# The running sum of a width-31 convolution moves from SBUF to a PSUM bank

## The chip, the cores and the metric

The kernel runs on one core of a Trainium2 chip. The metric is device time in microseconds of one execution. A core has a matmul engine (TensorE, PE in the profile; PEld are its weight loads), a vector engine (VectorE, DVE), a scalar engine (ScalarE, ACT), a third engine for elementwise work (GpSimd, POOL) and a sequencer that here only issues DMAs (SP). Matmul results go to PSUM, of which the kernel uses eight banks of 128 partitions x 512 floats; all other tiles lie in SBUF.

## What is computed

One layer of a decoder trunk over 1024 tokens of width 1024, in float32:

```python
h = x * (1.0 + sc1) + sh1                       # shift and scale from an adaLN projection of c
proj = h @ w_in                                 # 5136 columns
conf_val, conf_gate, z, xbc, dt_raw = split(proj)
u = conf_val * sigmoid(conf_gate)
u = silu(layer_norm(causal_dwconv31(u) + b))    # depthwise, 31 taps, over 1024 channels
xbc = silu(causal_dwconv4(xbc))                 # depthwise, 4 taps
y = ssd_chunked(...)                            # Mamba-2 scan, chunks of 128, 16 heads in 4 groups
mix = concat([u, gated_rmsnorm(y, z)]) @ w_out
x = layer_norm(ALPHA * x + g1 * mix)
# then: a hierarchical mixture of 64 experts, two for each token, and a second layer norm
```

## The kernel before

Channels lie on the partitions and tokens along the free dimension. The tokens are worked through in two halves of 512 (`h` = 0 and 1). For each half, the projection runs in blocks of 128 columns: `proj` (L477) takes a PSUM bank and adds up 8 x 3 matmuls of 128x512 in it (L475; each float32 weight and input is split in a high and a low part, and three of the four products are taken). In the first half the weights come from HBM, are split by ACT (L448) and POOL (L449), and are stored as `wind`; the second half loads them from there.

A block of the wide convolution is in `conf_block` (L594). Its gate (`pg`) leaves its bank through ACT (L602), its value (`pv`) through DVE (L605), which also makes `u`. ACT sets the running sum `acc` to the last tap plus the bias (L609). Of the other 30 taps, the first three to five go to ACT and POOL (L614, L616); the rest are DVE's, one scalar_tensor_tensor for each (L620): `acc` = `u` shifted x weight + `acc`, 128x512. There are 16 such chains, eight in each half, 426 taps in all. POOL adds its part (L623).

PSUM is divided by tags: `mm` four banks, `ta` two, `ss` two. The projection's blocks use `mm`, and so do the adaLN accumulations (`ada`, L298 to L306): one of these runs for each third of that projection, two of them a few matmuls at a time between the blocks of the first half, each holding its bank from its first matmul to its last. The output projection (`out_mm`, L924) runs in four passes A to D of two token tiles; a pass needs four banks at once (`pms`), adds up 16 x 3 matmuls in each, and its banks are emptied by L969.

What is written here is a set of generators that are taken in turn; a scheduler then orders the instructions of each engine by its own model of their times. Each engine runs its list in order, so an instruction that waits holds up what stands behind it. After the output projection come routing tables and the experts, whose weights (`ring`) are streamed in.

## Time and profile before

| | |
|---|---|
| runs | 2160.04, 2157.35, 2159.57 us; median 2159.57 |
| profiled execution | 2157.99 us, of which the span of its instructions 2156.0 |
| mean granted clock of TensorE | 0.94 of full speed |
| busy: PE, DVE, ACT, POOL | 1826.5, 1073.0, 547.7, 619.1 us |
| L620, the taps | 426 instructions, 433.3 us busy, mean 1029 ns |
| written and read in HBM | 83.44 and 576.08 MB |

A busy engine is one with an instruction in flight. A stretch of the span is read by the engine that is fullest in it, and by who waits for whom; shares over the whole span mix stages with different limits. The name in front of an arrow is the tile that is written, those behind it are read. Where a wait is listed, the engine stood idle before that line until the other engine's line had finished.

### The profile page before, as it was taken

What the parts mean: (1) busy time and instruction counts of PE and PEld (TensorE: products, weight loads), DVE (VectorE), ACT (ScalarE), POOL (GpSimd) and SP (SyncE); (2) the same over time, 40 slices, a digit from 0 to 9 for tenths busy, and PEclk for the clock granted to TensorE, in tenths of its full rate; (3) what the DMA queues carried; (4) which work ended last, traced back from release to release, by engine and by line L of the source; (5) the groups of instructions that cost most, each with busy time, mean ns of one, the idle gap of its engine ahead of it and who ended that gap; (6) DMA issues with size and microseconds to landing.
All of it is one profiled execution on the core that took longest, in us unless ns stands there. A gap on an engine that the chain in (4) does not pass through costs nothing.

```text
span 2156.0 us, 23640 instructions
## 1 busy us (share of the span) xinstructions
PE 1826.5 (85%) x8135; PEld 1012.6 (47%) x8135; DVE 1073.0 (50%) x1796; ACT 547.7 (25%) x990; POOL 619.1 (29%) x440
## 2 busy tenths in 40 slices
PE   4897989689989999889678969989799897998784
PEld 1365656558667767767432313324234241433232
DVE  1499898977999999897830301000000000000036
ACT  0234535264344446443320000001000010000011
POOL 0345656651544346553510000100001000000014
PEclk7998999889989999999879999999999998999997
DMA  8877877646443425657489999899998999999964
GB/s 260 288 256 240 249 252 232 230 145 219 153 131 132 165 93 171 206 182 279 171 312 419 419 421 383 339 420 420 419 374 338 420 420 420 420 409 372 420 255 160
DMA packets 204278, 626.01 MB, mean 290 GB/s; under 512 B 25566, under 2 KB 91350, under 8 KB 157308
## 3 DMA queue, kind: packets, MB, share of 16 engines
q1 hardware_dynamic: 156080, 552.79, 66.9%
q10 hardware_dynamic: 36700, 46.51, 6.7%
q0 software_dynamic: 11376, 25.18, 3.3%
q8 instruction: 65, 1.06, 0.2%
q14 instruction: 57, 0.47, 0.1%
HBM read 576.08 MB, written 83.44 MB: 306 GB/s over the span
## 4 chain that ended last, share of the span: by engine, by line
PE 30%; DMA 26%; DVE 20%; issue 4%; ACT 2%; POOL 1%; ACTq 0%; SPq 0%; DVEq 0%; POOLq 0%
DMA ring<-in_expert_w_dram 24%; DVE acc L620 8%; PE mix L475 5%; PE h0h L1325 2%; PE h1h L1325 2%; PE ypl L1344 2%; PE yph L1344 2%; PE ypt L1344 1%; PE h1l L1325 1%; PE h0t L1325 1%; PE px L475 1%; PE h1t L1325 1%; PE h0l L1325 1%; DVE cy L694 1%; DVE ctl L950 1%
## 5 line engine op out<-in xcount | busy, mean ns | idle before, releaser
L620 DVE SCALAR_TENSOR_TENSOR acc<-u,cw,acc 128x512 f32<-128x512 f32 x426 | 433.3, 1029 | 17.5 <-ACT acc L609 13.5
L1290 POOL DMA_INDIRECT xg<-h2d,gidx x32 | 33.0, 1033 | 724.0 <-PE tph L1298 203.8
L475 PE MATMUL px<-hTh,wx_hl 128*128 128x512 f32 x512 | 175.3, 413 | 3.5 <-ACT wx_hl L448 3.0
L475 PE MATMUL mix<-wo_hl,cth 128*128 128x512 f32 x416 | 136.2, 421 | 14.9 <-DVE wo_hl L449 10.2
L1325 PE MATMUL h1s<-ring,xTs 128*32 128x512 f32 x512 | 99.3, 691 | 42.6 <-DMA ring<-in_expert_w_dram 42.6
L1344 PE MATMUL yps<-ring,hTs 128*32 128x512 f32 x512 | 109.5, 599 | 19.3 <-DMA ring<-in_expert_w_dram 16.9
L1331 DVE TENSOR_TENSOR s1s<-s1s,h1s 128x512 f32<-128x512 f32 x8 | 5.5, 688 | 223.2 <-PE h1s L1325 223.2
L475 PEld LDWEIGHTS px<-hTh,wx_hl 128*128 128x128 f32 x512 | 99.0, 195 | 36.0 <-ACT wx_hl L448 5.2
L475 PE MATMUL px<-hTl,wx_hl 128*128 128x512 f32 x256 | 105.1, 410 | 0.0
L475 PEld LDWEIGHTS mix<-wo_hl,cth 128*128 128x128 f32 x416 | 81.1, 199 | 38.4 <-DVE wo_hl L449 14.1
L449 POOL TENSOR_TENSOR wo_hl<-wo,wo_hl 128x512 fp32r<-128x512 f32 x52 | 76.1, 1473 | 60.5 <-ACT wo_hl L448 60.1
L305 PE MATMUL ada<-wada,cond 128*32 128x512 f32 x192 | 74.2, 673 | 21.9 <-DMA wada<-in_w_ada_dram 21.8
L475 PE MATMUL pg<-hTh,wg_hl 128*128 128x512 f32 x256 | 90.1, 419 | 1.9 <-ACT wg_hl L448 0.9
L1325 PE MATMUL h0s<-ring,xTs 128*32 128x512 f32 x512 | 75.6, 639 | 16.3 <-DMA ring<-in_expert_w_dram 16.3
L475 PE MATMUL pz<-hTh,wz_hl 128*128 128x512 f32 x256 | 86.2, 404 | 2.1 <-ACT wz_hl L448 1.1
L475 PE MATMUL mix<-wo_hl,ctl 128*128 128x512 f32 x208 | 80.3, 422 | 7.4 <-DVE ctl L950 7.3
L475 PE MATMUL pv<-hTh,wv_hl 128*128 128x512 f32 x256 | 85.7, 405 | 0.4 <-DVE h L514 0.4
L1325 PEld LDWEIGHTS h1s<-ring,xTs 128*32 128x32 f32 x512 | 22.0, 124 | 116.1 <-DMA ring<-in_expert_w_dram 75.3
L1349 DVE SCALAR_TENSOR_TENSOR ys<-yps,gslot,g_bc 128x512 f32<-128x512 f32 x16 | 12.0, 751 | 120.0 <-PE yps L1344 120.0
L448 ACT CAST wo_hl<-wo 128x512 fp32r<-128x512 f32 x104 | 63.1, 616 | 26.7 <-PE mix L475 14.7
L1344 PEld LDWEIGHTS yps<-ring,hTs 128*32 128x32 f32 x512 | 27.1, 109 | 87.5 <-issue 45.4
L1325 PE MATMUL h1l<-ring,xTl 128*64 128x512 f32 x256 | 63.1, 595 | 5.7 <-DMA ring<-in_expert_w_dram 5.7
(603 smaller groups left out, 3618.9 us busy)
## 6 DMA issues: line engine op xcount, KB each, us to landing
ring<-in_expert_w_dram SPq DMA_DIRECT2D x384, 1024.0 KB
wo<-in_w_out_dram SPq DMA_DIRECT2D x112, 256.0 KB
wada<-in_w_ada_dram SPq DMA_DIRECT2D x96, 256.0 KB
wind<-wx_hl SPq DMA_DIRECT2D x32, 512.0 KB
wx_hl<-wind SPq DMA_DIRECT2D x32, 512.0 KB
ybuf<-zeros ACTq DMA_DIRECT2D x8, 1024.0 KB
wind<-wg_hl SPq DMA_DIRECT2D x16, 512.0 KB
wind<-wv_hl SPq DMA_DIRECT2D x16, 512.0 KB
```

Of the source, the lines that this page charges most:

```text
L305: nc.tensor.matmul(pm[32 * j:32 * j + 32, :], lhs, wt, start=(k == 0), stop=(k == KT - 1), tile_position=(0, 32 * j))
L448: nc.scalar.copy(hi, wt)
L449: (eng or nc.gpsimd).tensor_tensor(lo, wt, hi, op=OP.subtract)
L475: nc.tensor.matmul(pt, lhs[a_], rhs[b_], start=(first and n == 0), stop=(last and n == 2))
L620: nc.vector.scalar_tensor_tensor(acc, u[:, j:j + HALF], cw[:, t, j:j + 1], acc, op0=OP.mult, op1=OP.add)
L694: nc.vector.scalar_tensor_tensor(acc, raw[:, j:j + HALF], sw[:, j, t:t + 1], acc, op0=OP.mult, op1=OP.add)
L950: nc.vector.tensor_tensor(cl, ck, ch, op=OP.subtract)
L1290: nc.gpsimd.indirect_dma_start(out=t_, out_offset=None, in_=h2d, in_offset=bass.IndirectOffsetOnAxis(ap=gcol, axis=0), bounds_check=T - 1, ...
L1325: nc.tensor.matmul(hp[a:b, :], xT[:, 4 * hf + k, a:b], w_[:, k, :], start=(hf + k == 0), stop=(hf + k == 4), tile_position=(0, a))
L1331: nc.vector.tensor_tensor(s1, s1, hps[1], op=OP.mult)
L1344: nc.tensor.matmul(yps[n][a:b, :], hT[:, 2 * hf + k, a:b], w_[:, k, 512 * n:512 * n + 512], start=(hf + k == 0), stop=(hf + k == 2), tile_ ...
L1349: nc.vector.scalar_tensor_tensor(y[:, half[n]], yps[n], gate, g2_bc[:, half[n]], op0=OP.mult, op1=OP.mult)
```

## The change

The pool `mm` goes from four banks to three, and a tag `ac` with one bank is new. In `taps`, the first DVE tap of a chain reads `acc` from SBUF and writes a tile in `ac`; the following ones read and write that tile; the last reads it and writes `acc` in SBUF. The transposes of the first half's start use `ac` for one of the banks that they had in `mm`. Passes A, C and D of the output projection take their fourth bank, or for C their second, from `ac`; B is as before.

```diff
--- before.py
+++ after.py
@@ -271,7 +271,11 @@
         wk = p0.enter_context(tc.tile_pool(name="wk", bufs=2, side="right"))
 
         def mm_bank(name):
-            return ps.tile([P, 512], F32, tag="mm", bufs=4, name=name)
+            return ps.tile([P, 512], F32, tag="mm", bufs=3, name=name)
+
+        def ac_bank(name):
+
+            return ps.tile([P, 512], F32, tag="ac", bufs=1, name=name)
 
         def ta_bank(name):
             return ps.tile([P, 512], F32, tag="ta", bufs=2, name=name)
@@ -482,7 +486,7 @@
 
         def make_h(h):
 
-            banks = [mm_bank] * 8 if h else [mm_bank] * 3 + [ta_bank] * 2 + [ss_bank] + [mm_bank] * 2
+            banks = [mm_bank] * 8 if h else [mm_bank] * 2 + [ac_bank] + [ta_bank] * 2 + [ss_bank] + [mm_bank] * 2
             hT = []
             tps = {}
 
@@ -591,6 +595,14 @@
             yield
             return v3(dt), v3(dtd), v3(cd), v3(nacs)
 
+        def taps(nm, acc, terms):
+
+            run_ = acc
+            for j, (v_, w_) in enumerate(terms):
+                to = acc if j == len(terms) - 1 else ac_bank(f"ac{nm}") if j == 0 else run_
+                nc.vector.scalar_tensor_tensor(to, v_, w_, run_, op0=OP.mult, op1=OP.add)
+                run_ = to
+
         def conf_block(h, hT, b):
             accs = []
             for s_ in range(2):
@@ -616,9 +628,7 @@
                         nc.gpsimd.tensor_tensor(side, side, tmp, op=OP.add)
                     else:
                         side = tmp
-                for j in range(m, 30):
-                    nc.vector.scalar_tensor_tensor(acc, u[:, j:j + HALF], cw[:, t, j:j + 1], acc,
-                                                   op0=OP.mult, op1=OP.add)
+                taps(f"{h}_{t}", acc, [(u[:, j:j + HALF], cw[:, t, j:j + 1]) for j in range(m, 30)])
                 if m:
                     nc.gpsimd.tensor_tensor(acc, acc, side, op=OP.add)
                 add_part(h, "m", MG, ME, t, acc)
@@ -924,7 +934,7 @@
         def out_mm(h, i0, cat_, banks):
 
             sl = slice(i0 * P, (i0 + 2) * P)
-            pms = [[bank(f"mix{h}_{i0 + i}_{n}") for n in range(2)] for i, bank in enumerate(banks)]
+            pms = [[bank(f"mix{h}_{i0 + i}_{n}") for n, bank in enumerate(pair)] for i, pair in enumerate(banks)]
             ks = list(range(16))
             if (h, i0) == (1, 2):
                 ks = ks[16 - NK:] + ks[:16 - NK]
@@ -1068,8 +1078,9 @@
         O2 = "LA B XA LB F C XB LC D XC LD XD".split()
         got = {}
         live = {}
-        passes = {"A": (0, 0, ok, (mm_bank, mm_bank)), "B": (0, 2, None, (ta_bank, mm_bank)),
-                  "C": (1, 0, ok, (mm_bank, ta_bank)), "D": (1, 2, None, (mm_bank, mm_bank))}
+        mm, ta, ma = (mm_bank, mm_bank), (ta_bank, ta_bank), (mm_bank, ac_bank)
+        passes = {"A": (0, 0, ok, (mm, ma)), "B": (0, 2, None, (ta, mm)),
+                  "C": (1, 0, ok, (ma, ta)), "D": (1, 2, None, (mm, ma))}
 
         def part(h, o_):
             k, n = o_[0], o_[1:]
```

The scheduler orders the whole program anew. On DVE, in the first half, where the convolution's blocks 2 and 3 meet (`acc_2` and `acc_3` are their sums in SBUF, `ac_2` and `ac_3` those in PSUM, `u_3` the input of block 3). Before:

```order
L605 SCALAR_TENSOR_TENSOR u_3_1247<-u_3_1247,pv_3_1249 128x512
L620 SCALAR_TENSOR_TENSOR acc_2_1101<-u_2_1071,cw,acc_2_1101 128x512
L607 COPY halo_u<-u_3_1247 128x30
L620 SCALAR_TENSOR_TENSOR acc_2_1101<-u_2_1071,cw,acc_2_1101 128x512
L620 SCALAR_TENSOR_TENSOR acc_3_1277<-u_3_1247,cw,acc_3_1277 128x512
L620 SCALAR_TENSOR_TENSOR acc_2_1101<-u_2_1071,cw,acc_2_1101 128x512
L620 SCALAR_TENSOR_TENSOR acc_3_1277<-u_3_1247,cw,acc_3_1277 128x512
```

And now:

```order
L617 SCALAR_TENSOR_TENSOR u_3_1250<-u_3_1250,pv_3_1252 128x512
L603 SCALAR_TENSOR_TENSOR ac_2_1113<-u_2_1073,cw,ac_2_1113 128x512
L619 COPY halo_u<-u_3_1250 128x30
L603 SCALAR_TENSOR_TENSOR ac_2_1113<-u_2_1073,cw,ac_2_1113 128x512 x9
L752 TENSOR_TENSOR xc_0_1431<-tr_0_1427,dt_778 128x256
L752 TENSOR_TENSOR xc_0_1461<-tr_0_1457,dt_778 128x256
L603 SCALAR_TENSOR_TENSOR acc_2_1103<-u_2_1073,cw,ac_2_1113 128x512
L603 SCALAR_TENSOR_TENSOR ac_3_1290<-u_3_1250,cw,acc_3_1280 128x512
```

Before, the taps of the two blocks alternate from here on; now block 2 is brought to its end, nine taps in a row, and block 3 begins behind its last.

On PE, later in the same half, where a piece of the second adaLN accumulation (`ada`) stands by the projection groups `px_10` and `px_14`. Before:

```order
L475 MATMUL px_10_2339<-hTl_4_421,wx_10_1_hl 128x512
L305 MATMUL ada_1580<-wada_52_2429,cond 32x512
L475 MATMUL px_14_2444<-hTh_0_393,wx_14_0_hl 128x512
L475 MATMUL px_10_2339<-hTh_4_417,wx_10_1_hl 128x512
L755 MATMUL y_1_2180<-dec_1_2166,xc_1_2176 64x128 x4
L764 MATMUL sp_1_2189<-xd_1_2185,bt_1_2187 128x256
```

And now:

```order
L479 MATMUL px_10_2345<-hTh_7_445,wx_10_1_hl 128x512
L747 MATMUL tr_1_2388<-ident,cy_2_1413 128x128
L748 MATMUL tr_1_2388<-ident,cy_3_1519 128x128
L749 MATMUL tr_1_2388<-ident,bT_9_1629 128x128
L309 MATMUL ada_1584<-wada_52_2435,cond 32x512
L309 MATMUL ada_1584<-wada_53_2438,cond 32x512
L479 MATMUL px_14_2450<-hTh_0_393,wx_14_0_hl 128x512
```

Before, `px_14` opens its bank while `px_10` and `ada` hold theirs, three at once; now it opens behind the last matmul of `px_10`. Over both halves the projection groups start in the same order as before, with other places for the small matmuls between them.

## Rows read from the trace of the kernel before

**Rows 1.** The busy time of each engine in seven stretches of the span. Columns: from and to (us), length, then busy us and number of instructions in brackets for PE, PEld, DVE, ACT and POOL, then the granted clock of TensorE, the DMA share and GB/s.

```profile
0.00:85.00 85.00, 46.83 (x134) 13.84 (x134) 16.31 (x74) 11.19 (x17) 8.79 (x14) 0.80 0.87 271
85.00:108.00 23.00, 22.58 (x89) 15.53 (x89) 16.67 (x17) 6.11 (x10) 13.46 (x11) 1.00 0.83 286
108.00:432.00 324.00, 279.73 (x1233) 189.70 (x1232) 306.32 (x407) 135.60 (x236) 193.69 (x127) 0.93 0.75 243
432.00:486.00 54.00, 43.34 (x218) 32.47 (x216) 41.74 (x73) 31.61 (x55) 28.30 (x21) 0.87 0.45 143
486.00:810.00 324.00, 304.81 (x1537) 239.34 (x1536) 307.75 (x483) 143.59 (x252) 134.42 (x89) 0.96 0.44 149
810.00:1080.00 270.00, 226.15 (x1107) 179.05 (x1106) 235.09 (x451) 125.04 (x263) 144.75 (x86) 0.94 0.57 201
1080.00:2156.00 1076.00, 903.05 (x3828) 342.62 (x3828) 149.12 (x297) 94.59 (x158) 95.69 (x95) 0.95 0.94 379
```

**Rows 2.** The chain that ended last, shares of the span by line, from the page.

```profile
DMA ring<-in_expert_w_dram 24%; DVE acc L620 8%; PE mix L475 5%; PE h0h L1325 2%; PE h1h L1325 2%; PE ypl L1344 2%; PE yph L1344 2%; PE ypt L1344 1%; PE h1l L1325 1%; PE h0t L1325 1%; PE px L475 1%; PE h1t L1325 1%; PE h0l L1325 1%; DVE cy L694 1%; DVE ctl L950 1%
```

**Rows 3.** The order of time on DVE from 127.8 us. Columns: start, duration, engine, line, operation, output and inputs, shape, count.

```profile
127.81 1.78 DVE L620 SCALAR_TENSOR_TENSOR acc<-u,cw,acc 128x512 f32<-128x512 f32 x1
129.62 0.74 DVE L620 SCALAR_TENSOR_TENSOR acc<-u,cw,acc 128x512 f32<-128x512 f32 x1
130.28 0.74 DVE L694 SCALAR_TENSOR_TENSOR cy<-raw,sw,cy 128x512 f32<-128x512 f32 x1
130.94 1.78 DVE L620 SCALAR_TENSOR_TENSOR acc<-u,cw,acc 128x512 f32<-128x512 f32 x1
```

**Rows 4.** The same view of POOL beside it; the bracket is the idle time before.

```profile
127.37 1.67 POOL L449 TENSOR_TENSOR wx_hl<-wx,wx_hl 128x512 fp32r<-128x512 f32 x1 [1.56 <-ACT wx_hl L448]
130.72 1.44 POOL L449 TENSOR_TENSOR wx_hl<-wx,wx_hl 128x512 fp32r<-128x512 f32 x1 [1.68 <-ACT wx_hl L448]
```

**Rows 5.** The instructions that write or read the tile `u`, whole span; after the count stand the least, median and greatest duration in ns, then the first and last start in us.

```profile
L620 DVE SCALAR_TENSOR_TENSOR acc<-u,cw,acc x426: 643/752/2891, 96.7 to 808.1; 128x512 f32<-128x512 f32 x142
L605 DVE SCALAR_TENSOR_TENSOR u<-u,pv x16: 674/681/690, 95.2 to 764.2; 128x512 f32<-128x512 f32 x16
```

**Rows 6.** Groups of DVE's instructions by line and shape, whole span. Columns: line, operation, tiles, shape, count, then busy us and mean ns, then idle us before them and what ended it.

```profile
L620 DVE SCALAR_TENSOR_TENSOR acc<-u,cw,acc 128x512 f32<-128x512 f32 x426 | 433.3, 1029 | 17.5 <-ACT acc L609 13.5
L694 DVE SCALAR_TENSOR_TENSOR cy<-raw,sw,cy 128x512 f32<-128x512 f32 x48 | 48.0, 999 | 5.1 <-ACT cy L692 5.0
L514 DVE TENSOR_SCALAR h<-xT,sc,sh 128x512 f32<-128x512 f32 x16 | 12.4, 802 | 5.7 <-ACT hTh L506 5.3 <-POOL hTl L516 0.2
L790 DVE SCALAR_TENSOR_TENSOR cy<-cy,vcol,rss 128x512 f32<-128x512 f32 x16 | 11.2, 740 | 4.3 <-PE rss L651 4.3
L1564 DVE SCALAR_TENSOR_TENSOR ring<-z,mv,ring 128x512 f32<-128x512 f32 x9 | 6.7, 749 | 0.2
L1572 DVE SCALAR_TENSOR_TENSOR ring<-ring,rs,ring 128x512 f32<-128x512 f32 x7 | 5.2, 743 | 0.0
```

**Rows 7.** The busy time of L620 alone in three of the stretches. Columns: stretch, length, DVE busy and count, granted clock, DMA share, GB/s.

```profile
108.00:432.00 324.00, 212.40 (x196) 0.93 0.75 243
432.00:486.00 54.00, 10.02 (x12) 0.87 0.45 143
486.00:810.00 324.00, 199.96 (x210) 0.96 0.44 149
```

**Rows 8.** The busy time of L475, the projection's matmuls, in the two halves. Columns: stretch, length, PE busy and count, PEld busy and count, granted clock, DMA share, GB/s.

```profile
108.00:432.00 324.00, 212.80 (x814) 153.39 (x813) 0.93 0.75 243
486.00:810.00 324.00, 244.83 (x958) 182.21 (x958) 0.96 0.44 149
```

**Rows 9.** The chain that ended last in order of time: one piece of it, with start, length and what ran.

```profile
487.40 7.00 PE px L475 x30
```

**Rows 10.** Who PE waited for between 108 and 810 us: total us, times, longest us.

```profile
PE tr L744 <- DVE xc L742: 18.4, 6, 6.6
PE rss L651 <- DVE rs_y L173: 12.4, 4, 4.5
PE y L755 <- DVE dec L746: 11.0, 4, 4.0
PE acs L573 <- DVE a L569: 9.7, 2, 6.1
```

**Rows 11.** Who ACT waited for between 108 and 432 us: total us, times, longest us.

```profile
ACT cy L696 <- DVE cy L694: 34.7, 7, 6.8
ACT wx_hl L448 <- DMA wx<-in_w_in_dram: 25.3, 9, 5.7
ACT acc L609 <- DVE u L605: 24.1, 4, 10.7
ACT raw L688 <- DMA catd<-cy: 13.0, 1, 13.0
ACT wx_hl L448 <- DVE acc L620: 10.8, 1, 10.8
ACT cy L696 <- DVE raw L687: 8.3, 1, 8.3
ACT cT L696 <- DVE cT L694: 7.2, 1, 7.2
```

**Rows 12.** Groups of ACT's instructions between 108 and 432 us, one of those that empty a projection's bank: columns as in rows 6.

```profile
L688 ACT COPY raw<-px 128x512 f32<-128x512 f32 x15 | 8.7, 577 | 19.6 <-DMA catd<-cy 13.0 <-PE px L475 6.7
```

## The prediction

> **What bounds the kernel now.** I read the table of stages first [rows 1]. Seven stretches of the span: a start-up to 85 us; the first half of the tokens up to about 432; a change of half to 486; the second half to 810; the output projection to 1080; then the experts for 1076 us, where the DMA share is 0.94. Nothing of the change lies in the last stretch: it begins when the output projection is done and is as long as its weight stream. So whatever is won before 1080 should come off the end one for one, and nothing else can.
>
> In the two halves DVE is the fullest engine: 306.3 of 324 us and 307.8 of 324, both 95%. PE is close behind: 279.7 (86%) and 304.8 (94%). The reader is to see that this is not one bound but two near each other; what is taken from DVE is paid out only until PE is the limit. The chain that ended last agrees: the running sum of the wide convolution, L620, is its costliest compute group, 8% of the span, some 170 us [rows 2].
>
> Then I asked why one tap (one multiply-add of L620) costs 1.03 us on average, when its median is 0.752 [rows 5, 6]. The order of time shows two kinds: taps of 0.74 and taps of 1.78 [rows 3]. The long ones, at 127.81 and 130.94, begin while a POOL instruction with two SBUF inputs runs (127.37 to 129.04, 130.72 to 132.16) [rows 4]; the 0.74 ones begin while POOL is idle. The conv of width 4, also all in SBUF, averages 0.999 [rows 6]. L605, the same operation with its second input in PSUM, ran 16 times in the same stretches within 0.674 to 0.690: never held up [rows 5]. L790, also with its second tensor in PSUM, averages 0.740 [rows 6].
>
> **The change part by part.**
>
> Taps. 426 stay 426. The first of each of 16 chains still reads two SBUF tensors; the other 410 read the sum from PSUM, and all but the last of a chain write it there. The trace has no DVE write to PSUM, so I bound a tap: below by L605 (0.681), above by 1.03, no gain. Uncontended rows with a pointer scalar, as a tap has, stand at 0.740 (L790), 0.743 (L1572, all SBUF), 0.749 (L1564, from PSUM) and, the dearest, 0.802 (L514, from PSUM, two scalars) [rows 6]. I take 0.745. First half: 196 taps, 212.4 us busy [rows 7]; 188 x 0.745 + 8 x 1.08 = 149, so 63 less, DVE 306 to 243. Second half: 210 taps, 200.0; 202 x 0.745 + 8 x 0.95 = 158, 42 less, DVE 308 to 266. Between 432 and 486 there are 12 taps of 0.84: 1 us. Between 85 and 108 PE is busy 22.6 of 23 us: nothing. DVE loses 106 us in all. With 0.681 it would be 132, with 0.802 83, with 1.03 none.
>
> What is late next. PE needs its matmuls at the dense pace: 30 projection matmuls in 7.00 us, 0.233 each [rows 9]. The first half has 814 of them in 212.8 us, at a granted clock of 0.93 over the stretch; at the dense pace 190, so PE could do the half in 279.7 - 23 = 257. The second: 958 in 244.8, dense 223.5, so 304.8 - 21 = 284 [rows 1, 8]. These are floors: at most 67 and 40 us can go, 107 together. The waits that PE shows for DVE, 18.4 + 12.4 + 11.0 + 9.7 = 52 us over both halves, are the part most surely removed [rows 10].
>
> I take the second half to keep PE as full as it is, 94%: 284/0.94 = 301, a gain of 23. In the first half I take half of the 67, 34: 290 us, PE at 89%. I don't take 94% there, for two reasons. DMA moves at a share of 0.75 over 324 us, 243 us of work: in 290 it is at 0.84, near the 0.83 to 0.87 of the start-up [rows 1], and weights will come later against the work. And banks.
>
> Banks. The projection's pool goes from four to three, and the adaLN accumulation holds one of them through most of the first half: in either program's order 29 of the half's 40 projections begin while it does. So these have two banks where there were three; after a projection of 24 matmuls (5.6 us) its bank must be empty within one other projection, not two. Emptying is short (0.58 on ACT [rows 12], 0.68 on DVE [rows 5]); what counts is what stands ahead of it in ACT's queue. Six lines of ACT's waits in this half have a longest one of 13.0, 10.8, 10.7, 8.3, 7.2 and 6.8 us [rows 11]; what they exceed 5.6 by sums to 23 us. Price 0 to 23, taken as part of the 33 that I leave on the table. Most of them wait for DVE, and shorten with it. In the second half three banks remain; cost 0, covered by 11 us of lookahead.
>
> Chains. Before, the taps of two channels could alternate; one bank means one chain after the other. DVE runs one instruction at a time, and the instruction behind a tap of 0.74 starts 0.66 us after it [rows 3], so 0; a wait for the PSUM write would be part of the tap's bound.
>
> Output projection. Each pass still has four banks (A and D three of the pool and the sum's one, C one and one); a pass waits for the same predecessors as before. A's last bank is free when the last tap is, which its order already follows. 0; if a bank came late, the boundary would cost four evictions, about 3 us.
>
> POOL loses its opponent in 410 places; it is busy 60% and 41% of the halves [rows 1], so I count nothing for it.
>
> Sum: -34 - 23 - 1 = -58 against the profiled execution's 2157.99 (span 2156.0 and 2.0 around it): **2100 us**. The median of the runs shown, 2159.57, is 1.6 above it.
>
> [...] The rows put a DVE operation from PSUM at 0.749 and the like one from SBUF at 0.743 (L1564, L1572): 6 ns apart [rows 6]. [...]
>
> **The rivals.**
>
> First, the whole saving arrives: PE reaches its floors, 107 us, 2051. For it: PE's idle time in the first half, 44 us, and the lowered clock, both come from waiting. Against: DMA and ACT's waits remain. 13%.
>
> Second, the first half is held by its weights, and only the second gains: -24, 2134. For it: ACT waits 25.3 us for input weights, and the DMA share is the highest of the compute stages [rows 1, 11]. Against: PE's listed waits for the weight splits are small beside those for DVE. 17%.
>
> Third, a tap in PSUM takes 0.80, as L514: DVE 253 and 277, so close to PE's floors that a further 10 us go in the interplay: 2110. 10%.
>
> Fourth, it doesn't do what it says: a write to PSUM and the dependent read after it take as long as the contended tap. DVE unchanged, banks 0 to 23: about 2160 to 2180. 4%.
>
> Fifth, slower: the missing bank. PE stops at the head of each projection until ACT has reached the eviction, at 40 projections of the first half, two banks deep. The six lines of ACT's waits total 98 us [rows 11]; if PE took over all of it, -58 + 98 = +40, 2198. It decides from 59% of them on. Against: half of these waits are for DVE work that gets earlier, and PE's projection groups start in the same order. 8%.
>
> [...]
>
> **How the numbers follow.** My forecast, 2085 to 2120, has 48%; the third rival lies inside its range. The range for 8 in 10 runs from 2045, just under the first rival, to 2150, above the second; the fourth and fifth lie outside. Faster by over 0.2% (about what can be told from no change here): the forecast, and the first three rivals, 88%. Within 0.2%: the mild end of the fourth, 3%. Slower: 9%.
>
> **What would show it.** L603's taps (the old L620) near 0.745 with a narrow spread; if their mean is over 0.85, the taps' term is wrong. DVE busy near 243 and 266 us in the halves. The last tap near 750 instead of 808, and the first expert matmul some 58 us earlier; the experts' stretch still near 1076. PE's waits for DVE under 20 us; if instead PE waits for ACT's evictions (raw, u, zs) for tens of us, it is the banks. If the second half is short and the first still over 310 with weights awaited, it is the second rival. A change in the output projection's 270 us would be a term that I left out.

## The result and the profile after

The changed kernel takes 2079.68 us, the median of its runs (2077.93 to 2082.68); the kernel before, run beside it, 2159.6. The ratio is 0.9633, with a 95% interval of 0.9617 to 0.965: 80 us less, where 58 were forecast. 2079.7 lies under the forecast's 2085 to 2120 and inside its 2045 to 2150 for 8 in 10.

To compare the two programs I use four marks that stand in both in the same order on PE: the first projection matmul, the last one of the first half, the last one of the second half, and the last `mix` matmul of the output projection. Two of them, in the order of time on PE of the changed kernel; the columns are start, duration, engine, line, operation, tiles, shape and count:

```profile
396.57 0.39 PE L479 MATMUL pz<-hTl,wz_hl 128*128 128x512 f32 x1
396.80 0.40 PE L479 MATMUL pz<-hTh,wz_hl 128*128 128x512 f32 x1
397.03 1.02 PE L668 MATMUL mean<-sum0m,avg_d 128*128 128x512 f32 x2
...
974.97 0.40 PE L479 MATMUL mix<-wo_hl,ctl 128*128 128x512 f32 x1
```

In the kernel before, the same last projection of the first half begins at 446.68:

```profile
446.68 0.39 PE L475 MATMUL pz<-hTh,wz_hl 128*128 128x512 f32 x1
```

All marks, for all kernels run (us; the total is the median, the ratio is against the kernel before run on the same chip):

| kernel | first projection | last of half 1 | last of half 2 | last `mix` | span | total, ratio and interval |
|---|---|---|---|---|---|---|
| before | 79.63 | 446.68 | 785.68 | 1053.49 | 2156.0 | 2159.6 |
| after | 86.20 | 396.80 | 713.68 | 974.97 | 2076.0 | 2079.7, 0.9633 (0.9617 to 0.965) |
| e1, banks only | 86.05 | 448.25 | 784.01 | 1051.51 | 2153.4 | 2149.5, 0.9959 (0.9945 to 0.9973) |
| e2, first half | 84.28 | 392.98 | 726.02 | 994.13 | 2096.0 | 2100.5, 0.9748 (0.9724 to 0.9771) |
| e3, second half | 85.20 | 447.39 | 767.13 | 1028.77 | 2131.8 | 2131.0, 0.9874 (0.9855 to 0.9892) |
| e4, alternate | 83.12 | 412.94 | 733.61 | 993.19 | 2100.1 | 2104.6, 0.9759 (0.9742 to 0.9776) |
| e5, less PE work | 87.72 | 399.15 | 700.23 | 973.79 | 2077.6 | 2079.1, 0.9641 (0.9625 to 0.9657) |
| e6, the same of before | 80.68 | 434.91 | 764.40 | 1051.23 | 2154.7 | 2156.9, 0.9995 (0.9982 to 1.0008) |
| e7, start-up | 78.63 | 393.25 | 712.92 | 976.55 | 2080.2 | 2080.7, 0.9647 (0.9631 to 0.9664) |
| e8, one tap more on DVE | 83.85 | 395.18 | 708.09 | 969.89 | 2072.6 | 2073.3, 0.961 (0.9591 to 0.9629) |
| e9, two banks | 87.00 | 416.30 | 726.34 | 1018.49 | 2122.2 | 2124.3, 0.9846 (0.983 to 0.9861) |
| e10, less DMA | 86.78 | 398.74 | 713.04 | 984.80 | 2224.3 | 2223.8, 1.0298 (1.0282 to 1.0314) |
| e11, e5 and e10 | 86.51 | 383.64 | 689.43 | 961.50 | 2195.1 | 2196.8, 1.0175 (1.016 to 1.0191) |
| e12, two taps more on DVE | 86.97 | 394.95 | 708.10 | 977.30 | 2077.9 | 2078.8, 0.9627 (0.9614 to 0.964) |

From the first two rows the 80 us are made up so. The first projection comes 6.6 later; from it to the last projection of the first half it is 310.6 us instead of 367.1, 56.5 less; from there to the last projection of the second half 316.9 instead of 339.0, 22.1 less; the output projection takes 261.3 instead of 267.8, 6.5 less; the rest 1.5 less. -80.0 in all.

Where the engines stand is seen in the stretches between these marks. First the kernel before, with the columns of [rows 1]:

```profile
85.00:450.00 365.00, 319.06 (x1411) 217.94 (x1411) 340.96 (x452) 155.40 (x269) 216.03 (x144) 0.93 0.75 245
450.00:786.00 336.00, 310.23 (x1588) 243.87 (x1587) 307.74 (x498) 147.37 (x255) 139.41 (x95) 0.95 0.44 149
786.00:1053.50 267.50, 239.27 (x1125) 187.58 (x1123) 234.27 (x439) 130.04 (x272) 141.53 (x87) 0.95 0.55 190
```

Then the same work after the change:

```profile
85.00:397.00 312.00, 307.76 (x1407) 211.33 (x1406) 274.86 (x447) 158.99 (x271) 190.71 (x144) 0.99 0.85 284
397.00:714.00 317.00, 305.18 (x1605) 241.52 (x1604) 280.51 (x508) 150.97 (x263) 119.43 (x96) 0.97 0.47 161
714.00:975.00 261.00, 236.45 (x1125) 186.21 (x1123) 223.78 (x433) 127.20 (x266) 136.99 (x85) 0.95 0.56 194
975.00:2076.00 1101.00, 910.79 (x3884) 348.22 (x3882) 172.85 (x338) 103.74 (x177) 113.45 (x102) 0.94 0.93 375
```

DVE gives back 66, 27 and 10 us, 104 in all; 63, 42 and 1 were forecast, 106, with stages cut at other times. In the first half PE is now busy 99% of the time (307.76 of 312) where it was 87%, at a granted clock of 0.99 instead of 0.93, and DVE falls to 88%. The DMA share rises from 0.75 to 0.85, as the forecast had it.

The taps, by line L603 (the old L620); after the count stand the least, median and greatest duration in ns, then the first and last start in us, as in [rows 5]:

```profile
L603 DVE SCALAR_TENSOR_TENSOR ac<-u,cw,ac x394: 674/751/925, 103.6 to 723.8; 128x512 f32<-128x512 f32 x197
L603 DVE SCALAR_TENSOR_TENSOR ac<-u,cw,acc x16: 749/1095/2523, 102.8 to 692.8; 128x512 f32<-128x512 f32 x16
L603 DVE SCALAR_TENSOR_TENSOR acc<-u,cw,ac x16: 735/744/749, 129.9 to 725.5; 128x512 f32<-128x512 f32 x16
```

The reader is to see three kinds. 394 taps read and write PSUM: none took over 925 ns, where one of before could take 2891. The last of each chain reads PSUM and writes SBUF: 744. The first of each chain reads two SBUF tensors and writes PSUM, and is as uneven as the old ones.

POOL's own order of time, set beside that of the taps, shows whose hold they were freed from. Before, 137 of the 426 taps took over 0.9 us, and every one of them began while a POOL instruction ran; the 277 that didn't begin so took 0.74 in the mean and 755 ns at most. After, 174 of the 394 taps that read and write PSUM began so too; they took 0.75 in the mean, like the rest, and one of them over 0.9, the one of 0.925.

What PE waited for in the first half before the change, 85 to 450 us (total us, times, longest us; the 52 us of [rows 10] are for both halves):

```profile
PE tr L744 <- DVE xc L742: 16.5, 4, 6.6
PE y L755 <- DVE dec L746: 7.4, 2, 4.0
PE rss L651 <- DVE rs_y L173: 7.0, 2, 4.5
PE acs L573 <- DVE a L569: 6.1, 1, 6.1
```

That is 37 us for DVE. After the change, 85 to 400 us, the whole list is:

```profile
PE ada L309 <- DMA wada<-in_w_ada_dram: 3.5, 1, 3.5
PE y L765 <- DVE dec L756: 2.3, 1, 2.3
PE px L479 <- ACT zs L724: 1.5, 1, 1.5
PE acs L577 <- DVE a L573: 0.4, 1, 0.4
```

The first of these lies before the first projection, at 84.35. And the wait has turned round; DVE's own longest line there is a wait for PE (1.7 us for the same line before):

```profile
DVE u L617 <- PE pv L479: 21.9, 4, 12.8
DVE state L780 <- POOL state L779: 2.5, 2, 2.0
```

### The profile page after: what moved, and what is told of

Read it like the earlier page. It is cut to its first block, busy times and chain, and to the rows that moved or that the text cites. A ratio compares the mean times of both kernels' runs of the same rounds, so it can differ in the third digit from the quotient of the medians.

```text
span 2076.0 us, 23660 instructions
## 1 busy us (share of the span) xinstructions
PE 1807.1 (87%) x8135; PEld 999.0 (48%) x8135; DVE 968.7 (47%) x1796; ACT 551.6 (27%) x992; POOL 569.8 (27%) x440
## 4 chain that ended last, share of the span: by engine, by line
PE 30%; DMA 23%; DVE 7%; issue 3%; ACT 1%; POOL 1%; ACTq 0%; SPq 0%; DVEq 0%; POOLq 0%
DMA ring<-in_expert_w_dram 20%; PE mix L479 4%; PE h0h L1336 3%; PE h1h L1336 3%; PE yph L1355 2%; PE ypl L1355 2%; PE h1l L1336 2%; PE yps L1355 2%; PE h0l L1336 1%; PE ypt L1355 1%; PE h0t L1336 1%; PE h1t L1336 1%; DMA yb<-ybuf 1%; DVE wo_hl L453 1%; PE h0f L1336 1%
## 5 line engine op out<-in xcount | busy, mean ns | idle before, releaser
L603 DVE SCALAR_TENSOR_TENSOR ac<-u,cw,ac 128x512 f32<-128x512 f32 x394 | 295.7, 751 | 5.6
L479 PE MATMUL px<-hTh,wx_hl 128*128 128x512 f32 x512 | 170.7, 404 | 1.5 <-ACT zs L724 1.5
L479 PE MATMUL mix<-wo_hl,cth 128*128 128x512 f32 x416 | 133.2, 418 | 11.3 <-DVE wo_hl L453 7.2
L309 PE MATMUL ada<-wada,cond 128*32 128x512 f32 x192 | 80.0, 665 | 25.6 <-DMA wada<-in_w_ada_dram 25.5
L1355 PE MATMUL ypl<-ring,hTl 128*64 128x512 f32 x256 | 66.6, 598 | 2.2 <-ACT hTl L1348 2.2
```

What stands on the lines that cost most here:

```text
L309: nc.tensor.matmul(pm[32 * j:32 * j + 32, :], lhs, wt, start=(k == 0), stop=(k == KT - 1), tile_position=(0, 32 * j))
L479: nc.tensor.matmul(pt, lhs[a_], rhs[b_], start=(first and n == 0), stop=(last and n == 2))
L603: nc.vector.scalar_tensor_tensor(to, v_, w_, run_, op0=OP.mult, op1=OP.add)
L1355: nc.tensor.matmul(yps[n][a:b, :], hT[:, 2 * hf + k, a:b], w_[:, k, 512 * n:512 * n + 512], start=(hf + k == 0), stop=(hf + k == 2), tile_ ...
```

## The experiments

My theory after reading this: the gain is wholly the taps' freedom from POOL, by the side they read; the missing bank costs nothing; and PE is what limits the halves now. Rivals: the banks or the new order on PE bring part of it; the side written is what matters; DVE or the weights' DMA still hold the halves.

**e1, the banks without the sum.** The pool of three, the transposes and the passes as changed, but every tap back in SBUF:

```diff
-                to = acc if j == len(terms) - 1 else ac_bank(f"ac{nm}") if j == 0 else run_
+                to = acc
```

> Pool of three banks, the sum's bank used by the transposes of the first half and by the passes, but the running sum itself stays in SBUF. Theory (the gain is the taps' freedom from POOL, and the missing bank costs nothing): the time of before plus the 6.6 us that the start-up lost, 2166 (2155 to 2176), taps again near 1.03 us in the mean, DVE 306 and 308 of the halves. Rival that the new order of PE's work or the banks themselves brought a part of the 80 us: 2150 or less. Rival that the missing bank costs and the faster taps hid it: 2185 or more.

0.9959, 2149.5 us: shorter than the theory allows, just inside the rival's bound. The taps are the old ones:

```profile
L603 DVE SCALAR_TENSOR_TENSOR acc<-u,cw,acc x426: 648/752/2889, 101.2 to 806.4; 128x512 f32<-128x512 f32 x142
```

So the missing bank costs nothing that can be measured here, where DVE sets the pace and PE has time to spare, and some 9 of the 80 us (0.4%) go with the banks or with the order they bring. Its profiled execution is its longest (span 2153.4) and shows only 2.6 of them, so where they lie stays open. Whether the bank costs something where PE sets the pace, e1 can't show; in the changed kernel PE's list above has 1.5 us for an eviction. The late start of 6.4 us is made up before the first half ends (448.25 against 446.68): in this run, where DVE sets the pace, 1.6 us of it are left there.

**e2 and e3, one half at a time.** The sum in PSUM only in the first half, and only in the second:

```diff
-                to = acc if j == len(terms) - 1 else ac_bank(f"ac{nm}") if j == 0 else run_
+                to = acc if j == len(terms) - 1 or nm[0] == "1" else ac_bank(f"ac{nm}") if j == 0 else run_
```

(for e3, `"0"`.)

> The running sum lies in PSUM in the first half of the tokens alone. Theory (each half pays by itself, the first is worth 53 us at its end and 60 without the start-up's loss): 2106 (2098 to 2114), the first half some 292 us with PE at 98%, the second as before, 325 to 336. Rival that the first half's gain needs the second's, because what is won there is lost at the change of half: 2130 or more.

> The running sum lies in PSUM in the second half alone. Theory: start-up +6.6, second half -19, output projection -6.5, so 2141 (2132 to 2150). If the output projection's 6.5 us belong to the banks and not to the second half's taps, e2 has them as well and e1 too (2160). Rival that the second half's gain is the same 53 as the first's, since both have about 200 taps: 2110.

e2 takes 2.5% off (0.9748), e3 1.3% (0.9874). Of 2156.8, the before beside them, these are 54 and 27 us. e2 is inside its range, e3 1 us under its own, and both rivals fall. 54 + 27 less the 9 that both share is 72, against 79 by the ratio of the whole change. The halves pay nearly independently. Without those 9 they are worth 45 and 18, the first more than twice the second for about the same number of taps. e3 also settles the output projection: its stretch is 261.6 there (1028.77 - 767.13), 268.1 in e2 and 267.5 in e1, so the 6.5 us belong to the second half's taps. The likely place is the last of them: after the last projection the kernel before still had 14 to run, at 1.19 us each, the changed one 12, at 0.71, which is 8.1 us less for DVE. The two kernels' rows of L620 and L603 in that stretch:

```profile
786.00:1053.50 267.50, 16.60 (x14) 0.95 0.55 190
```

```profile
714.00:975.00 261.00, 8.49 (x12) 0.95 0.56 194
```

**e4, taps in turn.** Every other tap writes the sum back to SBUF, so half of them read two SBUF tensors and write PSUM, and half read PSUM and write SBUF:

```diff
-                to = acc if j == len(terms) - 1 else ac_bank(f"ac{nm}") if j == 0 else run_
+                to = acc if j == len(terms) - 1 or j % 2 else ac_bank(f"ac{nm}_{j}")
```

> Taps in turn: one reads two SBUF tensors and writes the sum to PSUM, the next reads the sum from PSUM and writes it to SBUF. Theory (two SBUF sources are what POOL holds up): the taps that read PSUM 0.75, those that write it 0.95 to 1.3, DVE gives back half of its 106 us less, 53; 2105 to 2130. Rival (it is the write to SBUF that waits): the taps that write PSUM 0.75, those that write SBUF near 1.0, about the same total time. Rival (either side in PSUM is enough): both 0.75 and 2080.

The view of line L603 in e4:

```profile
L603 DVE SCALAR_TENSOR_TENSOR ac<-u,cw,acc x206: 675/760/2625, 99.7 to 744.6; 128x512 f32<-128x512 f32 x103
L603 DVE SCALAR_TENSOR_TENSOR acc<-u,cw,ac x206: 728/743/750, 100.5 to 745.6; 128x512 f32<-128x512 f32 x103
```

and its groups, with busy us and mean ns:

```profile
L603 DVE SCALAR_TENSOR_TENSOR ac<-u,cw,acc 128x512 f32<-128x512 f32 x206 | 200.3, 972 | 9.9 <-ACT acc L621 7.4
L603 DVE SCALAR_TENSOR_TENSOR acc<-u,cw,ac 128x512 f32<-128x512 f32 x206 | 152.8, 742 | 2.8
```

2104.6 us is at the low edge of the range. There are 206 taps of each kind, in the same stretches, beside the same POOL work (14 more, the ends of odd chains, lie all in SBUF). Those that read PSUM are never held up (742 ns in the mean, 750 at most); those that read two SBUF tensors are (972 in the mean, up to 2625), though they write PSUM. The side read decides, the side written doesn't, and the rivals of this run fall.

**e9, a second bank taken.** Two banks for the projections, the freed one given to another group, and the banks of the passes and of the first half's transposes changed to fit:

```diff
-            return ps.tile([P, 512], F32, tag="mm", bufs=3, name=name)
+            return ps.tile([P, 512], F32, tag="mm", bufs=2, name=name)
...
-            return ps.tile([P, 512], F32, tag="ss", bufs=2, name=name)
+            return ps.tile([P, 512], F32, tag="ss", bufs=3, name=name)
```

> The changed kernel with a further bank taken from the projections' pool, two instead of three (the group ss gets it); while the adaLN sum holds one of them, through most of the first half, each projection must be emptied before the next can begin. Theory (with two banks for the projections, as after the change, every eviction fits under the next projection, so the change paid nothing for its bank, but with one it can't): the first half's 29 projections beside the adaLN sum each pay an eviction of 0.6 to 0.7 and the wait in ACT's or DVE's queue, 1 to 3 us each, 30 to 90 us in all: 2110 to 2170. Rival (the bank is worth nothing at all here, since other groups' instructions fill PE): 2080.

2124.3, 45 us above the changed kernel: inside the expected range, but not for its reason. 19.5 of them lie before the last projection of the first half (416.30 against 396.80), 2/3 of a microsecond for each of the 29 projections beside the adaLN sum, where 1 to 3 were expected; the second half is 7 us shorter; 31 come in the output projection. Those 31 are in one line of PE's waits there (726 to 1019 us), for a step of the routing on DVE:

```profile
PE pos L885 <- DVE r_sm L913: 31.0, 2, 15.5
```

The changed kernel waits 0.7 us for `pos` there in all: `mix` matmuls stand on PE between the logits (`lg`) and `pos`, where e9 has none. In e9 the passes take banks of `ss`, the group of `pos`; that a pass therefore can't begin before `pos` is a reading of the edit that no run tests. Of the 19.5, PE's idle time is 7.4: in 85 to 417 us it is busy 320.4 of 332, so idle 11.6, against 4.2 in the changed kernel. Its waits for ACT's evictions are 5.8 us instead of 1.5. The rest is work in another order: 1459 matmuls stand in that stretch instead of 1407, and 46 fewer in the second half. So by these rows the first bank cost PE 1.5 us of waiting at most, and the second some 7 of idle time.

**e5, e6, e10, e11: what limits it now.** e5 takes work from PE: of the pz projections' three products one is left out.

```diff
...
-                mm3(pt, wt[k], hT[k], k == 0, k == KT - 1)
+                mm3(pt, wt[k], hT[k], k == 0, k == KT - 1, ((0, 0), (0, 1)) if name[:2] == "pz" else ((0, 0), (0, 1), (1, 0)))
```

e6 is the same edit in the kernel before.

> The changed kernel, but the 16 pz projections leave out their third product (the low part of the weights' split against the high part, 8 matmuls each): 128 matmuls at 0.233, 30 us less work on PE, DVE's work as it is. Theory (after the change PE is the limit of both halves, 98.5% and 98%): 20 to 30 us off 2080, so 2050 to 2060. Rival (DVE, at 92% and 93% of the same stretches, or the weights at a DMA share of 0.86 are at their limit too): 10 us or less, 2070 and more.

> The same 128 matmuls left out of the kernel before. Theory (there DVE is the limit): 0 to 10 us, 2150 to 2160. Rival (before the change too PE and DVE shared the limit): half of 30 or more, 2145 and less.

Both give nothing: e5 0.9641 against 0.9633 of the whole change, e6 0.9995. For e6 that was the theory, but its marks don't bear out that DVE alone was the limit: its halves end 11.8 and 21.3 us earlier than before the change (434.91 and 764.40), its last tap 14.7 earlier (793.4 against 808.1), and only the output projection gives all but 2.3 back. So before the change too, time taken from PE was paid within the halves. For e5 it was the rival, and the theory that PE is the limit seemed to fall. But the marks of e5 are odd: no gain in the first half (399.15), 15.8 us in the second (301.1 against 316.9), and 12.3 given back in the output projection. I added up, from the order of time on PE between 85 us and the last projection of the first half, the time from each matmul's start to the next one's. Projections fell from 241.1 us to 225.9, the 15 us that were taken out; the adaLN products `ada` rose from 36.1 to 46.6. I read this as a wait for their weights. e10 and e11 test that: the changed kernel and e5, both with less DMA.

```diff
-                        nc.sync.dma_start(wt, w_ada[k * P:(k + 1) * P, r * 2048 + j * 512:r * 2048 + (j + 1) * 512])
-                        nc.tensor.matmul(pm[32 * j:32 * j + 32, :], lhs, wt,
-                                         start=(k == 0), stop=(k == KT - 1), tile_position=(0, 32 * j))
+                        wd = 256 if r else 512
+                        nc.sync.dma_start(wt[:, 0:wd], w_ada[k * P:(k + 1) * P, r * 2048 + j * 512:r * 2048 + j * 512 + wd])
+                        for c0 in range(0, 512, wd):
+                            nc.tensor.matmul(pm[32 * j:32 * j + 32, c0:c0 + wd], lhs, wt[:, 0:wd],
...
```

> The changed kernel, with half of the adaLN weights of the two later thirds left out: 64 loads carry 128 KB instead of 256 and PE reads the same 256 columns twice, so the adaLN values are not the reference's and PE's work is the same. 8.4 of some 89 MB of the first half go. Theory (in e5's first half the 15 us taken from PE were eaten by the adaLN products' waits for their weights, 36.1 to 46.6 us, so DMA stands just behind PE): alone, with PE at its work for 292 us, 3 to 8 us off the first half, its last projection at 389 to 394 instead of 396.8. Rival (DMA sets the first half's length by itself): 9% of it, 25 us or more off, at 372 and less. Rival (DMA plays no part): none.

> What e5 and e10 leave out, together. Theory (PE and the weights are two limits a few us apart in the first half): now the first half does get shorter by the 15 us of the products left out and more, its last projection at 374 to 382, where e5 had 399. Rival (a third thing, DVE or an order of steps, held e5's first half): 392 or more. The end: the stretch from the last projection to the last matmul of the output projection gave back 12 us in e5; if that is work on DVE or a chain of steps, it will give back as much here, 2060 to 2072; if it were PE's, 2050.

Their stretch of the experts is longer (1239.5 and 1233.6 us after the last `mix`, 1101.0 in the changed kernel), since other adaLN values choose other experts for the tokens, I take it; so I read them up to the last `mix` only. e10 alone gains nothing in the first half (398.74, where 389 to 394 were expected): DMA isn't the limit, and the theory it was to test is wrong in that point. e11's last projection, at 383.64, is 1.6 outside its theory's range as well. But e11 against e10 is the cleaner pair: their edits differ by the left-out products alone, and their order on PE is more alike than that of e5 and the changed kernel (of the first half's runs of like-named matmuls 87% stand in the same order in both, against 48%). The last projection of the first half in e10:

```profile
398.74 0.39 PE L482 MATMUL pz<-hTh,wz_hl 128*128 128x512 f32 x1
```

and in e11:

```profile
383.64 0.40 PE L482 MATMUL pz<-hTl,wz_hl 128*128 128x512 f32 x1
```

15.1 us earlier, for 64 matmuls of 0.233, 14.9; 23.6 at the last projection of the second half, 23.3 at the last `mix`, of 29.8. PE's idle time in the first half is about the same in both (11.3 us of 314 and 10.7 of 299), its busy time 14.5 less. So PE does limit the first half, one for one, and most of the second.

What e5 lost there is in the order of its matmuls, not in the DMA. Two rows of the changed kernel show an adaLN run of two and one of four, each with the instruction behind it:

```profile
171.73 1.04 PE L309 MATMUL ada<-wada,cond 128*32 128x512 f32 x2
172.71 0.50 PE L479 MATMUL pg<-hTh,wg_hl 128*128 128x512 f32 x1
...
205.24 1.05 PE L309 MATMUL ada<-wada,cond 128*32 128x512 f32 x4
206.22 0.44 PE L765 MATMUL y<-dec,xc 128*64 128x128 f32 x4
```

Both hold PE for 0.98 us, as do 18 of the half's 22 runs of two and all 17 of four: in these, four products cost what two cost. The other four runs of two, at 113 to 117 us, held it for 0.03 to 0.53 us. The changed kernel has 40 such runs in the first half, 17 of them of four; e5, whose matmuls the scheduler put in another order, 47, with 11 of four; e11, in matmuls of half the width, 31. Counted from the first projection to the last of the half, the `ada` products take 36.2, 44.8 and 33.3 us. From the changed kernel to e5 that is 8.5 more, with a wait of 2.7 for DVE (`xc`) behind one run among them. (The 46.6 above holds 1.8 from before e5's first projection.) The small matmuls of the scan and the sums take 7.5 more: 3.1 are `mean` products, which in the changed kernel stand behind the half's last projection, and the rest is in `y`, `tr` and `sp`. With 15.2 less for the projections and a start 1.5 later this makes up e5's 2.3 us. PE waits for no DMA in e5 once its projections have begun. No run changes the order alone, so this is argued from these counts. Why e5's output projection takes 12 us more stays open: more of the last scan's steps (96 `y` products against 64, 22 `tr` against 20) stand behind the last projection there, and the same count puts 2.7 us on `y`, 3.6 on `tr` and 3.6 on `mix`.

**e7, the start-up.** The seventh transpose takes a bank of another group, and PE has three pairs of adaLN matmuls between the transposes and the first projection again, not five:

```diff
-            banks = [mm_bank] * 8 if h else [mm_bank] * 2 + [ac_bank] + [ta_bank] * 2 + [ss_bank] + [mm_bank] * 2
+            banks = [mm_bank] * 8 if h else [mm_bank, mm_bank, ac_bank, ta_bank, ta_bank, ss_bank, ss_bank, mm_bank]
```

> The changed kernel with the seventh transpose of the first half in a bank of the group ss instead of one of the pool of three: on PE three matmuls of the adaLN sum, not five, then stand ahead of the first projection, as before the change. Theory (PE is the limit from there on, so the late start of its projections counts): first projection at 80 again, 4 to 7 us off, 2073 to 2076. Rival (the late start is made up, as e1 had it, whose half ended at 450.1 in spite of it): no difference, 2080.

The first projection is back at 78.6, the first half ends 3.5 us earlier, and at the last `mix` it is 1.6 later: 2080.7, no difference. (By the marks e1's half ended at 448.25, not at 450.1.) The theory fails for the whole: of the 7.6 us won at the first projection 3.5 are left at the end of the first half, 0.8 at the end of the second and none after the output projection.

**e8 and e12, how much room DVE has.** One tap more of each chain on DVE, then two:

```diff
-TAPS = [[int(c_) for c_ in ("33333333" if h == 0 else "34553433")] for h in range(2)]
+TAPS = [[int(c_) for c_ in ("22222222" if h == 0 else "23442322")] for h in range(2)]
```

(for e12, `"11111111"` and `"12331211"`.)

> The changed kernel with one tap of each of the 16 chains moved from ACT and POOL to DVE: DVE 16 times 0.75, 12 us more, POOL some 45 us less. Theory (DVE has room since the change): within 5 us of 2080. Rival (DVE is still the limit beside PE): 12 us longer, 2092. If ACT or POOL hold a part of the path: a few us shorter.

> The changed kernel with two taps of each chain moved from ACT and POOL to DVE, one more than e8: DVE 24 us more than after the change, near 295 of 315 us in the second half. Theory (e8's 12 us more on DVE cost nothing because DVE waited that long for PE): with 24 the room is used up, 2075 to 2085, no better than e8's 2073. Rival (POOL is what held the change back, DVE isn't near its limit): shorter again by 5 or more, 2068. Rival (DVE is the limit of the second half): 2090.

e8's 2073.3 is 6.4 us under the changed kernel, 1.4 more than the theory allows; its interval (0.9591 to 0.9629) overlaps with that of the change, so I don't call it faster. e12's 2078.8 is inside its range. But they test less than was meant. The taps do take 12 and 24 us more (16 and 32 more of 0.751), while DVE's busy time over the whole execution is 968.7 us in the changed kernel, 977.9 in e8 and 976.5 in e12: 9.2 and 7.8 more, so in e12 the rest of DVE's work got some 16 us shorter. In e12's second half DVE is busy 283.7 of 313 us, not 295 of 315. POOL falls from 569.8 to 547.1 and 531.8, 23 us for the first tap, not 45. So some 9 us more of DVE's time cost nothing, and DVE is not the limit within that; before the change, time taken from its taps was paid, as e2 to e4 show. How much room it has beyond, and what POOL's shorter work adds, stays open.

## Why the prediction came out as it did

**The taps: right.** 0.745 was taken, 751 ns measured for 394 of them and 744 for the last ones; the bound of no gain, 1.03, and the dear value 0.80 (the third rival) are out. DVE gave back 104 us of 106. The first tap of a chain was taken at 1.08 and 0.95; its mean is 1.31 (20.9 us for 16), some 5 us more in all. A tap that reads and writes PSUM takes 751 against 743 for the uncontended all-SBUF row L1572 [rows 6], 8 ns more. In DVE's order of time the next tap of the same chain starts 0.79 us after such a tap (157 pairs, 0.77 at least), any other instruction 0.66 in the median (237): by these starts one chain after the other, priced at 0, takes an estimated 0.13 us of DVE's time for each pair. DVE idles 5.6 us in all before those 394.

**The first half: mechanism right, size wrong.** This is the term that was mis-sized: "In the first half I take half of the 67, 34: 290 us, PE at 89%." It gave 50 us at its last projection, 56 from its first to its last. Of the two reasons for taking half, neither held. The weights: the DMA share rose to 0.85, as worked out, and PE waited 3.5 us for a weight in all, before the first projection; e10 shows that less DMA brings nothing. The banks, priced at 0 to 23: PE waited 1.5 us for ACT's evictions in the half, e1 shows no cost where DVE sets the pace, and only one bank fewer still (e9) brings some 7 us of idle time. So PE ran at 99%, not 89%, and the floor worked out from the dense pace, 67, was the better guide; the second half's 94% would have been nearer too.

That floor was 44 us of idle time and 23 of matmuls brought to the dense pace. By the rows of the stretches, idle time fell from 45.9 us (365 less 319.06) to 4.2 (312 less 307.76), by 41.7, nearly all of it. PE's busy time for the same work fell by 11.3, half of the 23, at a granted clock that rose from 0.93 to 0.99. So the waits were the larger part, and the shorter busy time at the higher clock the smaller. In the kernel before, three stretches of 25 us in this half:

```profile
160.00:185.00 25.00, 17.00 (x60) 10.62 (x61) 24.82 (x34) 7.92 (x14) 15.12 (x10) 0.80 0.71 233
...
210.00:235.00 25.00, 19.34 (x80) 12.62 (x82) 25.00 (x34) 6.01 (x10) 15.99 (x10) 0.80 0.56 173
...
385.00:410.00 25.00, 15.53 (x64) 12.03 (x64) 25.00 (x25) 6.55 (x12) 18.56 (x9) 0.79 0.79 272
```

DVE is full, PE sits at 15 to 19 of 25 us, and the mean clock of the stretch is 0.79 to 0.80. After the change the clock of the half is 0.99. From start to start a projection matmul took 0.300 us before and 0.251 after, 0.233 being the dense pace [rows 9]; for the 959 of them between the marks that is 46.5 us, most of what the half gained. 39 of these are idle time behind such a matmul, 43.2 us before and 4.2 after; without it the matmuls took 0.255 and 0.247, 7.5 us. Taking away the wait gave the wait, 39 us, and, on top, these 7.5 at the higher clock; the dense pace was not reached.

**The second half: right in size, by another sum.** -23 was forecast, -22.1 measured at its last projection. The forecast had 21 us less of busy time, at the dense pace, and PE as full as before. By the rows, PE's busy time fell by 5.1 (310.23 to 305.18) and its idle time by 14.0 (25.8 to 11.8): PE went from 92% to 96%, and the gain was mostly waits, as in the first half. That the two sums agree is luck.

**The output projection: 0 was forecast, -6.5 came.** A term that was left out by where the stage was cut: the last taps lie behind the last projection, and e3 shows that the gain goes with the second half's taps. The forecast's stage ended at 810, behind the last tap (808.1 before, 725.5 after). Reckoned to that tap, the second half gave 32.7 us, more than the 23, and the output projection takes 245.4 and 249.5, so 4 more.

**The start-up: 0 was forecast, +6.6 came** at the first projection, from two more pairs of adaLN matmuls ahead of it, the last behind the 3.5 us wait for its weight. e7 shows that undoing it wins nothing at the end.

**The experts: right,** 1102.5 and 1101.0 after the last `mix`. POOL was counted at nothing. Its busy time fell by 49 us (619.1 to 569.8) for the same 440 instructions; what that is worth stays open, as e8 does.

**The rivals.** The first, PE at its floors (2051), was nearer in the first half than the forecast, but the second half never reached its 40. The second fell with the first half's 56 us, and e10 shows no gain from less DMA. The fourth fell with the taps' rows. The fifth, 98 us of waits moved to PE, has become 1.5 us of PE waiting for ACT.

## What to carry to other kernels

Where a long chain on DVE reads two SBUF tensors beside a busy POOL, put the running operand in PSUM: here it was the side read that counted (e4: 742 ns with the sum read from PSUM, 972 with two SBUF inputs), and the write could go to either (751 to PSUM, 744 to SBUF). When an engine stops being waited for, reckon the follower's idle time as gone unless a row shows another wait (41.7 of 45.9 us here), and the dense pace only in part (11.3 of 23). And an edit that takes work out of a scheduled program changes the order too: compare two variants that share the order, or count the pieces, before calling an engine not the limit.

## What was not expected

In 18 of the changed kernel's 22 runs of two in the first half, two adaLN products in a row hold PE as long as four do, 0.98 us, so how the scheduler breaks them up has a price: 36.2 us in the changed kernel's first half, 44.8 in e5's, a wait of 2.7 included. And the banks alone, with a start 6.4 us later and no faster tap, made the kernel 0.4% shorter (0.9945 to 0.9973); no profile here shows where.
